# Two gates of five channel blocks by seven products, in one fused diffusion-transformer layer

## The chip, the core and the metric

One core of a Trainium2 chip. The kernel is one launch; its time is the device time in microseconds. TensorE (PE) multiplies, VectorE (DVE) and ScalarE (ACT) work elementwise, GpSimd (POOL) too, SyncE (SP) issues most loads. PEld is the loading of a matmul's stationary operand.

## The reference

One layer over x of 512 tokens by 1024 channels; everything is float32. The part that the change touches is the merge of three branches (Fourier f, convolution cv, attention at) under three gates, and the sums that give the modulation vectors:

```python
mod = jax.nn.silu(c) @ ada_w[l] + ada_b[l]
sh1, sc1, g1, sh2, sc2, g2 = jnp.split(mod, N_MOD, axis=-1)
hx = modulate(rmsnorm(x, norm1_g[l]), sh1, sc1)
px = split_proj(hx @ w_in[l])          # px[7], px[8], px[9]: the three gates, 1024 wide each
m = (jax.nn.sigmoid(g_f) * (f @ w_f) + jax.nn.sigmoid(g_c) * (cv @ w_c)
     + jax.nn.sigmoid(g_a) * (at @ w_a))
x = x + g1 * (m @ w_o)
x = x + g2 * sq_relu_mlp(modulate(rmsnorm(x, norm2_g[l]), sh2, sc2), mlp_w1[l], mlp_w2[l])
return rmsnorm(x, final_g)
```

## The kernel before

Every operand of a product is split into a high and a low part (split: ACT casts the high one, L59, DVE subtracts the low one, L60), and one product of a 128x128 weight piece with 512 tokens is three matmuls (mm3: L82 high by high, L83 high by the moving low, L84 the weight's low by the moving high). Weights come in 512 KB loads (weights(), L65 on SP) into two raw tiles (wraw) and are split into three tiles (wsp).

The stages in time: norm and values to 100 us, Fourier, convolution and attention to 241, the gates and merge to 402, output projection wO and second norm to 470, MLP to 790. In the attention, head() puts turns (four transposes tp and the split into pth and ptl, L421) on a list called pending, and output() (the matmuls po) closes a head; the three gates of block 0 are computed in between as filler, and drain() runs what is left.

The gate stage runs over 8 channel blocks c of 128 channels. In each, three gates of 24 matmuls of 512 columns (pg, moving operand hx), a sigmoid each on ACT, a merge of 24 (pbr, 6 for f, 6 for cv, 12 for at), products and sums on DVE (L536 to L538), and a split into mT. Among them DVE does 32 modulation units (ada_unit, L513): a 128x1024 block of ada_w, times a column of sig, added to acc, four vectors q of eight k each: q = 0 is g1, 1 the shift and 2 the scale of norm 2, 3 is g2. They start from a memset of acc on POOL (L507). In the first half of wO (py, four quarters kk, weights loaded by L65), a spread per q sums acc over the partitions by matmuls with ones (4 each).

In the MLP, two hidden blocks at a time are already computed by seven products (class Pair): with the moving operand and the weights cut in two by two quarters, seven products of quarter sums stand in for eight, each of 12 matmuls of 256 columns. The weights' sums are made by POOL (L768 to L773) and split again.

The order on each engine follows the written program, except that a scheduling layer moves instructions of one engine ahead of others that would wait. Buffers of a pool are reused in turn, so a load waits for the last reader of its tile.

Of the kernel before, what the change touches and what calls it, by code (L numbers as in the profile page):

```python
# [10 lines left out]
F32 = mybir.dt.float32  # L11
# [26 lines left out]
def dit_block(ctx: ExitStack, tc: tile.TileContext, a: dict):  # L38
# [16 lines left out]
    def f(ap):  # L55
        return ap.bitcast(F32)
# [345 lines left out]
    def head(p, j, q, bt, ats):  # L402
# [111 lines left out]

    ada_todo = [(k, q) for q in range(4) for k in range(KD)]
    for c in range(KD):
        pgs = []
        for b in range(3):
            if c == 0:
                sg = raw_gates[b]  # L520
                S.activation(sg, sg, AF.Sigmoid)
            else:
                pg = psG.tile([P, 512], F32, tag="g", name="pg")
                proj(pg, weights(a["wG"][c, b]))
                sg = (gp if c % 2 else sgp).tile([P, SEQ], F32, tag="sg", name="sg")
                S.activation(sg, pg, AF.Sigmoid)  # L526
            pgs.append(sg)
            ada_unit(*ada_todo.pop(0))
        w = weights(a["wM"][c])
        pbs = []  # L530
# [331 lines left out]
    def finish(pd, t, lo, n):  # L862
# [29 lines left out]
    for j, p in pairs.items():  # L892
# [150 lines left out]
```

## Time and profile before

| | us |
|---|---|
| median of 3 runs (804.94 to 805.08) | 805.07 |
| the profiled execution, its own time | 804.62 |
| its span, first to last instruction | 802.8 |
| PE busy | 783.9 |
| DVE busy | 528.2 |
| ACT busy | 347.0 |
| POOL busy | 110.6 |

The span is 1.8 us below the profiled execution's time, which holds what lies around the instructions. Busy times are of the whole span; what a stage is limited by is read from the windows of that stage. The durations of matmuls overlap: a matmul's cost is the distance between two starts.

### The profile page before, as it was taken

The page shows a single profiled execution, that of the slowest core. Times are in us where ns is not written, and L with a number is a line of the kernel's source. Part 1 is how long each engine was busy: PE and PEld are TensorE (multiplying, and loading weights), DVE is VectorE, ACT ScalarE, POOL GpSimd, SP SyncE. Part 2 cuts the span into 40 slices and gives each one's busy share as a digit, 9 for nine tenths or more (in the row PEclk, how much of TensorE's full clock was granted, in tenths as well). Part 3 has the DMA queues.
Part 4 walks back from the last instruction along what each step waited for, and adds up shares of the span by engine and source line. Part 5 has one row for each costly group of instructions (what it writes and reads, how often), then busy time and mean ns, then how long its engine had stood idle before and what let it go on. Part 6 is the DMA issues. An engine that isn't in the chain of part 4 may idle for free.

```text
span 802.8 us, 11393 instructions
## 1 busy us (share of the span) xinstructions
PE 783.9 (98%) x4484; PEld 674.4 (84%) x4484; DVE 528.2 (66%) x792; ACT 347.0 (43%) x587; POOL 110.6 (14%) x124
## 2 busy tenths in 40 slices
PE   5999999999999999999999999999999999999996
PEld 4779988788878888888888999999889989998885
DVE  4555445997888888543358988656556666475963
ACT  5434435564772222322245475344543444334232
POOL 1000011221210000000000005222221222032000
PEclk9999999999999999999999999999999999999999
DMA  8653242332308897322444142223233333221312
GB/s 342 249 198 94 84 126 67 85 94 79 83 28 296 311 324 248 131 83 102 151 146 150 39 146 80 86 99 110 101 106 106 106 105 105 105 79 53 119 65 106
DMA packets 33528, 104.07 MB, mean 130 GB/s; under 512 B 8001, under 2 KB 8129, under 8 KB 33473
## 3 DMA queue, kind: packets, MB, share of 16 engines
q1 hardware_dynamic: 32834, 100.99, 36.8%
q0 software_dynamic: 640, 2.36, 1.5%
q8 instruction: 35, 0.57, 0.3%
q14 instruction: 19, 0.16, 0.1%
HBM read 98.87 MB, written 2.10 MB: 126 GB/s over the span
## 4 chain that ended last, share of the span: by engine, by line
PE 94%; DVE 2%; ACT 1%; issue 1%; DMA 1%; SPq 0%; POOLq 0%; POOL 0%; ACTq 0%
PE pd L82 7%; PE pd L83 7%; PE pd L84 7%; PE pg L84 5%; PE pg L83 5%; PE pg L82 5%; PE pA L84 3%; PE pA L83 3%; PE pA L82 3%; PE pu L83 2%; PE pu L82 2%; PE pu L84 2%; PE pbr L83 2%; PE pbr L84 2%; PE pbr L82 2%; PE vacc L82 2%
## 5 line engine op out<-in xcount | busy, mean ns | idle before, releaser
L60 DVE TENSOR_TENSOR w<-raw,w 128x1024 fp32r<-128x1024 f32 x87 | 108.1, 1243 | 51.7 <-ACT w L59 51.7
L59 ACT CAST w<-raw 128x1024 fp32r<-128x1024 f32 x87 | 91.2, 1048 | 75.9 <-PE pbr L84 27.7
L60 DVE TENSOR_TENSOR w<-rr,w 128x512 fp32r<-128x512 f32 (+1 forms) x65 | 66.6, 1044 | 70.8 <-ACT w L59 69.6
L83 PE MATMUL pd<-w,aT 128*128 128x512 f32 x224 | 87.8, 392 | 0.0
L84 PE MATMUL pd<-w,aT 128*128 128x512 f32 x224 | 87.6, 391 | 0.0
L82 PE MATMUL pd<-w,aT 128*128 128x512 f32 x224 | 85.8, 394 | 0.0
L59 ACT CAST w<-rr 128x512 fp32r<-128x512 f32 (+1 forms) x65 | 45.0, 707 | 77.2 <-POOL rr L772 34.7
L84 PE MATMUL pg<-hx,w 128*128 128x512 f32 x192 | 76.4, 398 | 0.0
L83 PE MATMUL pg<-hx,w 128*128 128x512 f32 x192 | 76.2, 397 | 0.0
L82 PE MATMUL pg<-hx,w 128*128 128x512 f32 x192 | 74.9, 390 | 0.0
L84 PEld LDWEIGHTS pd<-w,aT 128*128 128x128 f32 x224 | 42.0, 188 | 9.3
L83 PEld LDWEIGHTS pd<-w,aT 128*128 128x128 f32 x224 | 42.1, 188 | 8.9 <-DVE w L60 0.8
L82 PEld LDWEIGHTS pd<-w,aT 128*128 128x128 f32 x224 | 41.8, 188 | 8.2 <-ACT w L59 0.4
L513 DVE SCALAR_TENSOR_TENSOR acc<-ada,sig,acc 128x1024 f32<-128x1024 f32 x32 | 40.9, 1282 | 10.1 <-DMA ada<-in_adaB 9.6
L82 PEld LDWEIGHTS pg<-hx,w 128*128 128x128 f32 x192 | 36.8, 192 | 8.0
L83 PEld LDWEIGHTS pg<-hx,w 128*128 128x128 f32 x192 | 36.1, 188 | 7.9
L768 POOL TENSOR_TENSOR rr<-rr 128x512 f32<-128x512 f32 x13 | 17.3, 1332 | 183.4 <-DVE w L60 159.9
L84 PEld LDWEIGHTS pg<-hx,w 128*128 128x128 f32 x192 | 36.1, 188 | 7.3
L104 POOL TENSOR_TENSOR ss<-ss,mhalf 128x1 f32<-128x1 f32 x10 | 6.6, 658 | 242.8 <-DVE ss L103 242.8
L526 ACT ACTIVATE sg<-pg 128x512 f32<-128x512 f32 x21 | 12.5, 597 | 62.2 <-PE pg L84 62.1
L536 DVE TENSOR_TENSOR sg<-pbr,sg 128x512 f32<-128x512 f32 x24 | 16.5, 686 | 20.6 <-PE pbr L84 20.6
L84 PE MATMUL pA<-Sq,w 128*128 128x256 f32 x104 | 29.3, 282 | 0.0
(337 smaller groups left out, 2152.1 us busy)
## 6 DMA issues: line engine op xcount, KB each, us to landing
raw<-in_w SPq DMA_DIRECT2D x38, 512.0 KB, 3.4
ada<-in_adaB SPq DMA_DIRECT2D x32, 512.0 KB, 4.6
rr<-in_w SPq DMA_DIRECT2D x26, 512.0 KB, 4.0
raw<-in_wG SPq DMA_DIRECT2D x24, 512.0 KB, 3.4
raw<-in_adaA SPq DMA_DIRECT2D x16, 512.0 KB, 5.5
raw<-in_wM SPq DMA_DIRECT2D x8, 512.0 KB, 3.4
raw<-in_wO SPq DMA_DIRECT2D x8, 512.0 KB, 3.3
raw<-in_wC SPq DMA_DIRECT2D x6, 512.0 KB, 3.3
```

Of the source, the lines that this page charges most:

```text
L59: S.copy(hi, src)
L60: V.tensor_tensor(lo, src, f(hi), op=ALU.subtract)
L82: PE.matmul(out, st[0], mv[0], start=start, stop=False, **kw)
L83: PE.matmul(out, st[0], mv[1], start=False, stop=False, **kw)
L84: PE.matmul(out, st[1], mv[0], start=False, stop=stop, **kw)
L104: G.tensor_tensor(ss, ss, mhalf[:, 0:n], op=ALU.pow)
L513: V.scalar_tensor_tensor(acc[:, q, :], raw, sigv[:, k, 0:1], acc[:, q, :], op0=ALU.mult, op1=ALU.add)
L526: S.activation(sg, pg, AF.Sigmoid)
L536: V.tensor_tensor(pgs[b], pb, pgs[b], op=ALU.mult)
L768: G.tensor_tensor(ra[:, lo], ra[:, lo], rb[:, lo], op=ALU.add)
```

## The change

For blocks 0 to 2 the gates stay as they are. For blocks 3 to 7 (FIRST = 3) the first two gates are computed as one pair of seven products, 84 matmuls of 256 columns (class Gates) in place of 48 of 512; the third gate and the merge keep theirs. Four quarter sums of hx (Sg0 to Sg3, gate_sums) are made on DVE and split during blocks 0 to 2, in memory of acc and of tiles that the pairs use later. Each pair has four additions of 128x512 on POOL for the weights' sums. The products run in the order gA, gC, gB, gA, gC, and then among the merge's parts: pbr of f, p7, pbr of cv, p4, pbr of at. The merge weights of these blocks lie in rows of mT that aren't filled yet, and those of block 7 in the two ada tiles.

The memset of acc is gone: the unit k = 0 of a vector writes acc (TENSOR_SCALAR, L520), and POOL's queue adds the bias to one partition by an accumulating load. Units are pinned to the written order; q = 3 (g2) moves to the MLP, eight units in pairs 4 to 11 and a spread in pair 13. Six units are left for after block 7. There are two ada tiles, before three. At the end of attention, the last output() goes through the list, and the last two turns are set into the middle of gate 2 of block 0.

The core of the diff:

```diff
...
-            if jb == 3:
+            if jb == 3 and (p, j) == (3, 1):
+                later(lambda: output(p, j, pth, ptl, ats))
+            elif jb == 3:
                 output(p, j, pth, ptl, ats)
...
-    def raw_gate(b):
+    def raw_gate(b, midway=None):
...
-        proj(pg, weights(a["wG"][0, b]))
+        w = weights(a["wG"][0, b])
+        proj(pg, w, ks=range(0, 4))
+        if midway:
+            midway()
+        proj(pg, w, ks=range(4, KD))
...
-            raw_gate(2)
+            raw_gate(2, lambda: [pending.pop(0)() for _ in range(2)])
...
-    gp = pool(gg, "gp", 3)
+    gp = pool(gg, "gp", 2)
+    gq = pool(gg, "gq", 1)
     psG = pool(gg, "psG", 8, space=PSUM)
-    G.memset(acc, 0.0)
-    nc.sync.dma_start(acc[0:1], a["adab"])
...
     def ada_unit(k, q):
         raw = gp.tile([P, D], F32, tag="ada", name="ada")
         nc.sync.dma_start(raw, a["adaB"][q, k])
-        V.scalar_tensor_tensor(acc[:, q, :], raw, sigv[:, k, 0:1], acc[:, q, :], op0=ALU.mult, op1=ALU.add)
...
-    ada_todo = [(k, q) for q in range(4) for k in range(KD)]
+        if k:
+            unit = V.scalar_tensor_tensor(acc[:, q, :], raw, sigv[:, k, 0:1], acc[:, q, :], op0=ALU.mult, op1=ALU.add)
+        else:
+            unit = V.tensor_scalar(acc[:, q, :], raw, sigv[:, 0, 0:1], None, op0=ALU.mult)
+        tc.keep_in_program_order(unit)
+        if k == 0:
+            G.dma_start(acc[0:1, q, :], a["adab"][:, q, :], accum_op=ALU.add)
...
+    ada_todo = [(0, q) for q in (0, 2, 1)] + [(k, q) for q in (0, 2, 1) for k in range(1, KD)]
...
+    def ada_some(n):
+        for _ in range(min(n, len(ada_todo))):
+            ada_unit(*ada_todo.pop(0))
...
+    def gate_sums():
...
+        whole(u, quarter(1, 0))
+        yield
+        whole(v, quarter(1, 1))
+        V.tensor_tensor(v, v, u, op=ALU.subtract)
+        keep(0, v)
+        yield
+        whole(w, quarter(0, 0))
+        V.scalar_tensor_tensor(v, v, -1.0, w, op0=ALU.mult, op1=ALU.subtract)
...
+        whole(w, quarter(0, 1))
+        V.scalar_tensor_tensor(w, v, -1.0, w, op0=ALU.mult, op1=ALU.subtract)
+        keep(3, w)
...
+    class Gates:
...
+        def __init__(self, c, sgs):
...
+            self.ra = wraw.tile([P, RAW], F32, tag="raw", name="ra")[:, :D]
+            nc.sync.dma_start(self.ra, a["wG"][c, 0])
+            self.rb = gq.tile([P, D], F32, tag="rb", name="rb")
+            nc.sync.dma_start(self.rb, a["wG"][c, 1])
+        def weights(self):
+            ra, rb = self.ra, self.rb
+            self.w1 = wsp.tile([P, 2, RAW], F32R, tag="w", name="w")
+            split(self.w1[:, 0, :D], self.w1[:, 1, :D], ra)
+            lo, hi = slice(0, 512), slice(512, 1024)
+            G.tensor_tensor(ra[:, lo], ra[:, lo], rb[:, lo], op=ALU.add)
+            self.b22 = gq.tile([P, 2, 512], F32R, tag="b22", name="b22")
+            split(self.b22[:, 0], self.b22[:, 1], rb[:, hi])
+            G.tensor_tensor(rb[:, lo], rb[:, lo], rb[:, hi], op=ALU.add)
+            G.tensor_tensor(rb[:, hi], ra[:, lo], rb[:, hi], op=ALU.add)
+            G.tensor_tensor(ra[:, hi], ra[:, hi], rb[:, hi], op=ALU.add)
+            self.w2 = wsp.tile([P, 2, RAW], F32R, tag="w", name="w")
+            split(self.w2[:, 0, lo], self.w2[:, 1, lo], ra[:, lo])
+            split(self.w2[:, 0, hi], self.w2[:, 1, hi], rb[:, hi])
...
+        def last_weights(self):
...
+            self.w3 = wsp.tile([P, 2, RAW], F32R, tag="w", name="w")
+            split(self.w3[:, 0, lo], self.w3[:, 1, lo], rb[:, lo])
+            split(self.w3[:, 0, hi], self.w3[:, 1, hi], ra[:, hi])
...
+        def first_products(self):
+            self.A, self.C, B = [psG.tile([P, 512], F32, tag="g", name=n) for n in ("gA", "gC", "gB")]
+            r0, r1 = self.sgs
+            self.product(self.A, self.w1, 0, quarter(0, 0), True)
+            a1 = self.copy("e1", self.A)
+            self.product(self.C, self.w2, 0, self.sq(0), True)
+            self.a5 = self.copy("e5", self.C)
+            self.product(B, self.w1, 512, quarter(0, 1), True)
+            V.tensor_tensor(r0[:, :HT], B[:, :HT], a1, op=ALU.add)
+            S.activation(r0[:, :HT], r0[:, :HT], AF.Sigmoid)
+            self.product(self.A, self.w2, 512, self.sq(1), False)
+            a2 = self.copy("e2", self.A)
+            self.last_weights()
+            self.product(self.C, self.b22, 0, self.sq(3), False)
+            V.tensor_tensor(r1[:, :HT], self.C[:, :HT], a2, op=ALU.add)
...
+        def p7(self):
+            r1 = self.sgs[1]
+            self.product(self.A, self.w3, 0, self.sq(2), False)
+            V.tensor_tensor(r1[:, HT:], self.A[:, :HT], self.a5, op=ALU.add)
+            S.activation(r1, r1, AF.Sigmoid, scale=-1.0)
+        def p4(self):
+            self.product(self.A, self.w3, 512, quarter(1, 1), False)
+            S.activation(self.sgs[0][:, HT:], self.A[:, :HT], AF.Sigmoid)
...
+    FIRST = 3
...
+    def merge_weights(c):
...
+        if c < FIRST:
+            w = weights(a["wM"][c])
+            return [[w[:, h, k * P:(k + 1) * P] for h in range(2)] for k in range(KD)]
+        raw = wraw.tile([P, RAW], F32, tag="raw", name="raw")
+        nc.sync.dma_start(raw[:, :D], a["wM"][c])
+        if c < KD - 1:
+            w = [mT[:, :, KD - 1 - h, :] for h in range(2)]
+        else:
+            w = [gp.tile([P, D], F32R, tag="ada", name="wm").rearrange("p (i n) -> p i n", i=2) for _ in range(2)]
+        split(w[0], w[1], raw[:, :D].rearrange("p (i n) -> p i n", i=2))
+        return [[w[h][:, k // 4, (k % 4) * P:(k % 4 + 1) * P] for h in range(2)] for k in range(KD)]
...
+    sums = gate_sums()
...
+        pair = c >= FIRST
+        for b in (2,) if pair else range(3):
+            if c in (1, 2):
+                next(sums, None)
...
+            if not pair:
+                ada_some(1)
+        if pair:
+            gates = Gates(c, pgs[:2])
+            gates.weights()
+            w = merge_weights(c)
+            gates.first_products()
+            ada_some(1 if c < KD - 1 else 0)
...
         for b, (k0, n, src) in enumerate(((0, 2, fT), (2, 2, cvT), (4, 4, atT))):
...
             for k in range(n):
-                mm3(pb, [w[:, h, (k0 + k) * P:(k0 + k + 1) * P] for h in range(2)],
-                    [src[:, h, k, :] for h in range(2)], k == 0, k == n - 1)
-            V.tensor_tensor(pgs[b], pb, pgs[b], op=ALU.mult)
+                mm3(pb, w[k0 + k], [src[:, h, k, :] for h in range(2)], k == 0, k == n - 1)
+            if pair and b < 2:
+                (gates.p7, gates.p4)[b]()
+            if pair and b < 1:
+                first = pb
+                continue
+            if b == 1 and pair:
+                V.tensor_tensor(pgs[1], pb, pgs[1], op=ALU.mult)
+                V.tensor_tensor(pgs[0], first, pgs[0], op=ALU.mult)
+            else:
+                V.tensor_tensor(pgs[b], pb, pgs[b], op=ALU.mult)
         V.tensor_tensor(pgs[0], pgs[0], pgs[1], op=ALU.add)
         V.tensor_tensor(pgs[0], pgs[0], pgs[2], op=ALU.add)
         split(mT[:, 0, c, :], mT[:, 1, c, :], pgs[0])
-        ada_unit(*ada_todo.pop(0))
+        ada_some((1, 0, 0, 1, 1, 1, 1, 24)[c])
...
-        q = (0, 2, 1, 3)[i]
+        q = (0, 2, 1)[i]
...
+        if kk < 3:
+            spread(kk)
...
+    G.memset(g2b, 0.0)
+    nc.sync.dma_start(g2b[0:1], a["adab"][:, 3, :])
...
+    def g2_unit(k):
+        raw = wraw.tile([P, RAW], F32, tag="raw", name="raw")[:, :D]
+        nc.sync.dma_start(raw, a["adaB"][3, k])
+        V.scalar_tensor_tensor(g2b, raw, sigv[:, k, 0:1], g2b, op0=ALU.mult, op1=ALU.add)
...
+        if 4 <= j < 12:
+            g2_unit(j - 4)
+        if j == 13:
+            g2_spread()
...
```

Three places of the order. The first is DVE from the last attention output (atT) to the low half of the weights of block 1's third gate (w_2573 before, w_2593 after). Numbers tell buffers apart; hx, u, w_2512 and Sg belong to the quarter sums. Before:

```order
L60 TENSOR_TENSOR atT_90<-ats_2129,atT_90 128x512
L536 TENSOR_TENSOR sg_2127<-pbr_2463,sg_2127 128x512
L513 SCALAR_TENSOR_TENSOR acc_2437<-ada_2447,sig_78,acc_2437 128x1024
L536 TENSOR_TENSOR sg_2356<-pbr_2471,sg_2356 128x512
L513 SCALAR_TENSOR_TENSOR acc_2437<-ada_2451,sig_78,acc_2437 128x1024
L537 TENSOR_TENSOR sg_2127<-sg_2127,sg_2356 128x512
L513 SCALAR_TENSOR_TENSOR acc_2437<-ada_2455,sig_78,acc_2437 128x1024
L536 TENSOR_TENSOR sg_2388<-pbr_2479,sg_2388 128x512
L60 TENSOR_TENSOR w_2573<-raw_2571,w_2573 128x1024
```

After (rows of block 0's merge are left out):

```order
L60 TENSOR_TENSOR atT_90<-ats_2129,atT_90 128x512
L550 TENSOR_TENSOR u_2511<-hx_88 128x1024
L520 TENSOR_SCALAR acc_2437<-ada_2452,sig_78 128x1024
L699 TENSOR_TENSOR sg_2127<-pbr_2471,sg_2127 128x512
...
L558 TENSOR_TENSOR acc_2437<-acc_2437,u_2511 128x1024
...
L60 TENSOR_TENSOR Sg0_2447<-acc_2437,Sg0_2447 128x1024
...
L550 TENSOR_TENSOR w_2512<-hx_88 128x1024
...
L518 SCALAR_TENSOR_TENSOR acc_2437<-ada_2505,sig_78,acc_2437 128x1024
L562 SCALAR_TENSOR_TENSOR acc_2437<-acc_2437,w_2512 128x1024
L518 SCALAR_TENSOR_TENSOR acc_2437<-ada_2545,sig_78,acc_2437 128x1024
L60 TENSOR_TENSOR Sg1_2448<-acc_2437,Sg1_2448 128x1024
...
L60 TENSOR_TENSOR w_2593<-raw_2591,w_2593 128x1024
```

Between atT and that split stood 7 rows; now 18 do: the quarter sums' five wide instructions and L562 have come in, and the units stand among them.

The second is DVE around block 4's merge. Before (w_3048 are the merge weights, w_3091, w_3126 and w_3161 the three gates of block 5):

```order
L60 TENSOR_TENSOR w_3048<-raw_3046,w_3048 128x1024
L60 TENSOR_TENSOR w_3091<-raw_3089,w_3091 128x1024
L536 TENSOR_TENSOR sg_2971<-pbr_3051,sg_2971 128x512
L60 TENSOR_TENSOR w_3126<-raw_3124,w_3126 128x1024
L536 TENSOR_TENSOR sg_3006<-pbr_3059,sg_3006 128x512
L537 TENSOR_TENSOR sg_2971<-sg_2971,sg_3006 128x512
L536 TENSOR_TENSOR sg_3041<-pbr_3067,sg_3041 128x512
L538 TENSOR_TENSOR sg_2971<-sg_2971,sg_3041 128x512
L60 TENSOR_TENSOR w_3161<-raw_3159,w_3161 128x1024
```

After, from the last splits of block 4's pair (w_3131) to L637, on which the pair's last product p4 waits, and the first product of its merge; w_3222 is the third gate of block 5, ra_3250 and rb_3252 are the raw weights of block 5's pair:

```order
L60 TENSOR_TENSOR w_3131<-rb_3051,w_3131 128x512
L60 TENSOR_TENSOR w_3131<-ra_3049,w_3131 128x512
L626 TENSOR_TENSOR sg_3015<-gB_3074,e1_3087 128x256
L60 TENSOR_TENSOR w_3222<-raw_3220,w_3222 128x1024
L632 TENSOR_TENSOR sg_3016<-gC_3073,e2_3129 128x256
L518 SCALAR_TENSOR_TENSOR acc_2437<-ada_3149,sig_78,acc_2437 128x1024
L60 TENSOR_TENSOR w_3254<-ra_3250,w_3254 128x1024
L60 TENSOR_TENSOR b22_3258<-rb_3252,b22_3258 128x512
L637 TENSOR_TENSOR sg_3016<-gA_3072,e5_3101 128x256
L696 TENSOR_TENSOR sg_3016<-pbr_3173,sg_3016 128x512
```

L637 has come in, behind a unit and two splits of the next pair; the merge's first product L536 (now L696) waits behind it.

The third is SP's queue at the start of wO. Before:

```order
L65 DMA raw<-in_wM 128x1024
L65 DMA raw<-in_wO 128x1024 x3
L564 DMA x_3535<-in_x 128x1024 x3
L561 DMA a2b<-in_norm_g 128x1024
L564 DMA x_3535<-in_x 128x1024
L65 DMA raw<-in_wO 128x1024
```

After:

```order
L654 DMA raw<-in_wM 128x1024
L65 DMA raw<-in_wO 128x1024 x3
L516 DMA ada<-in_adaB 128x1024 x2
L727 DMA x_3840<-in_x 128x1024
L516 DMA ada<-in_adaB 128x1024 x2
L727 DMA x_3840<-in_x 128x1024 x2
L516 DMA ada<-in_adaB 128x1024 x2
L727 DMA x_3840<-in_x 128x1024
L65 DMA raw<-in_wO 128x1024
```

Before, all units were done by then; now six unit loads and all x loads stand ahead of the fourth quarter of wO.

## Rows read from the trace of the kernel before

**Rows 1.** The page: busy time of each engine, and the chain by engine.
```profile
PE 783.9 (98%) x4484; PEld 674.4 (84%) x4484; DVE 528.2 (66%) x792; ACT 347.0 (43%) x587; POOL 110.6 (14%) x124
...
PE 94%; DVE 2%; ACT 1%; issue 1%; DMA 1%; SPq 0%; POOLq 0%; POOL 0%; ACTq 0%
```

**Rows 2.** Windows: length, busy us of each engine, clock, DMA share, GB/s.
```profile
225.00:241.00 16.00, 14.06 (x79) 11.20 (x78) 12.45 (x26) 10.79 (x21) 3.53 (x1) 1.00 0.11 35
243.00:270.00 27.00, 27.00 (x119) 22.08 (x118) 23.93 (x25) 7.34 (x10) 0.00 (x0) 1.00 0.91 319
270.00:404.00 134.00, 134.00 (x582) 109.70 (x581) 79.78 (x85) 38.27 (x49) 0.00 (x0) 1.00 0.53 183
404.00:427.00 23.00, 23.00 (x102) 18.80 (x101) 13.85 (x17) 10.76 (x15) 0.00 (x0) 1.00 0.43 147
427.00:470.00 43.00, 42.76 (x264) 37.72 (x263) 39.53 (x60) 21.60 (x41) 3.07 (x4) 1.00 0.23 76
```

**Rows 3.** Timeline of the end of attention: start, duration, instruction, [idle before, releaser].
```profile
228.30 3.53 POOL L507 MEMSET acc<- 128x4096 f32 x1 [12.98 <-issue]
...
230.21 1.90 DVE L444 TENSOR_SCALAR pr<-pr,mx 128x512 f32<-128x512 f32 x1
...
232.25 0.52 PE L421 MATMUL tp<-ident,pr 128*128 128x128 f32 x3 [0.83 <-DVE pr L444]
...
238.24 0.50 PE L452 MATMUL po<-pth,Vst 128*128 128x512 f32 x1 [0.78 <-ACT pth L59]
239.07 0.50 PE L452 MATMUL po<-ptl,Vst 128*128 128x512 f32 x1 [0.33 <-DVE ptl L60]
...
240.79 0.39 PE L82 MATMUL pbr<-fT,w 128*128 128x512 f32 x1
```

**Rows 4.** Windows of PE alone: one block of the MLP's products, one gate block.
```profile
487.62:499.05 11.43, 11.43 (x98) 1.00 0.35 120
333.00:355.18 22.18, 22.18 (x97) 1.00 0.29 95
```

**Rows 5.** Line L444: duration in ns, minimum/median/maximum, first and last start.
```profile
L444 DVE TENSOR_SCALAR pr<-pr,mx x32: 467/479/1898, 133.8 to 233.9; 128x512 f32<-128x512 f32 x32
```

**Rows 6.** Timeline of DVE at the start of the gates.
```profile
243.04 0.69 DVE L60 TENSOR_TENSOR atT<-ats,atT 128x512 fp32r<-128x512 f32 x1 [0.69 <-ACT atT L59]
...
244.89 1.28 DVE L513 SCALAR_TENSOR_TENSOR acc<-ada,sig,acc 128x1024 f32<-128x1024 f32 x1 [0.56 <-DMA ada<-in_adaB]
246.09 0.68 DVE L536 TENSOR_TENSOR sg<-pbr,sg 128x512 f32<-128x512 f32 x1
...
249.68 0.68 DVE L536 TENSOR_TENSOR sg<-pbr,sg 128x512 f32<-128x512 f32 x1
250.28 1.22 DVE L60 TENSOR_TENSOR w<-raw,w 128x1024 fp32r<-128x1024 f32 x1
251.42 0.69 DVE L538 TENSOR_TENSOR sg<-sg 128x512 f32<-128x512 f32 x1
```

**Rows 7.** Line L150, a wide DVE instruction with one SBUF tensor.
```profile
L150 DVE TENSOR_SCALAR xt<-xt,ss x6: 742/753/771, 7.8 to 26.3; 128x1024 f32<-128x1024 f32 x6
```

**Rows 8.** Loads: a unit load's first issue; KB each and median us to landing.
```profile
240.98 1.31 SPq L512 DMA_DIRECT2D ada<-in_adaB  x3
...
ada<-in_adaB SPq DMA_DIRECT2D x32, 512.0 KB, 4.6
...
q<-q POOLq DMA_DIRECT2D x8, 288.0 KB, 3.0
```

**Rows 9.** Timelines of POOL and of DVE in an MLP pair.
```profile
512.49 1.28 POOL L768 TENSOR_TENSOR rr<-rr 128x512 f32<-128x512 f32 x1 [11.47 <-DVE w L60]
513.85 1.63 POOL L771 TENSOR_TENSOR rr<-rr 128x512 f32<-128x512 f32 x1
...
512.66 1.67 DVE L60 TENSOR_TENSOR b<-rr,b 128x512 fp32r<-128x512 f32 x1
```

**Rows 10.** Lines of ACT from 382 to 430: busy, mean ns, idle before.
```profile
L59 ACT CAST w<-acc 128x1024 fp32r<-128x1024 f32 x4 | 4.2, 1046 | 10.4 <-PE py L84 10.4
```

More of the change, by code (lines that the diff above doesn't have):

```diff
@@ L252, in dit_block, with proj @@
     g1.close()
-    def proj(ps, w, src=hx):
-        for k in range(KD):
+    def proj(ps, w, src=hx, ks=range(KD)):
+        for k in ks:
             mm3(ps, [w[:, h, k * P:(k + 1) * P] for h in range(2)], [src[:, h, k, :] for h in range(2)],
@@ new lines, in ada_unit, with quarter @@
+        tc.keep_in_program_order(unit)
[5 more added lines that the diff above has]
+            ada_unit(*ada_todo.pop(0))
+    def quarter(i, j):
+        return [hx[:, h, 4 * j:4 * j + 4, i * HT:(i + 1) * HT] for h in range(2)]
+    Sg = [gq.tile([P, 2, 4, HT], F32R, name=f"Sg{i}") for i in range(4)]
@@ new lines, in half_tile, with whole, keep @@
+    def half_tile(n):
+        return n.rearrange("p (k t) -> p k t", t=HT)
+    def gate_sums():
+        u = half_tile(gq.tile([P, D], F32, tag="rb", name="u"))
+        v = half_tile(acc[:, 3, :])
+        w = half_tile(gq.tile([P, D], F32, tag="b22", name="w"))
+        def whole(dst, q):
+            V.tensor_tensor(dst, f(q[0]), f(q[1]), op=ALU.add)
+        def keep(i, src):
+            split(Sg[i][:, 0], Sg[i][:, 1], src)
+        whole(u, quarter(1, 0))
[6 more added lines that the diff above has]
+        V.scalar_tensor_tensor(v, v, -1.0, w, op0=ALU.mult, op1=ALU.subtract)
+        keep(1, v)
+        yield
+        V.tensor_tensor(u, w, u, op=ALU.subtract)
+        keep(2, u)
+        yield
+        whole(w, quarter(0, 1))
+        V.scalar_tensor_tensor(w, v, -1.0, w, op0=ALU.mult, op1=ALU.subtract)
+        keep(3, w)
@@ new lines, in dit_block, with product, sq, copy @@
+    class Gates:
+        def __init__(self, c, sgs):
+            self.c, self.sgs = c, sgs
+            self.ra = wraw.tile([P, RAW], F32, tag="raw", name="ra")[:, :D]
[17 more added lines that the diff above has]
+        def last_weights(self):
+            ra, rb = self.ra, self.rb
+            lo, hi = slice(0, 512), slice(512, 1024)
+            self.w3 = wsp.tile([P, 2, RAW], F32R, tag="w", name="w")
+            split(self.w3[:, 0, lo], self.w3[:, 1, lo], rb[:, lo])
+            split(self.w3[:, 0, hi], self.w3[:, 1, hi], ra[:, hi])
+        def product(self, bank, w, lo, mv, start):
+            for k in range(4):
+                c = lo + k * P
+                mm3(bank[:, :HT], [w[:, h, c:c + P] for h in range(2)], [mv[h][:, k, :] for h in range(2)],
+                    start and k == 0, k == 3, skip_group_check=True)
+        def sq(self, i):
+            return [Sg[i][:, h] for h in range(2)]
+        def copy(self, tag, bank):
+            e = gq.tile([P, HT], F32, tag=tag, name=tag)
+            S.copy(e, bank[:, :HT])
+            return e
+        def first_products(self):
[21 more added lines that the diff above has]
+            S.activation(self.sgs[0][:, HT:], self.A[:, :HT], AF.Sigmoid)
@@ L519, in dit_block @@
+    sums = gate_sums()
+    for c in range(KD):
+        pgs = raw_gates if c == 0 else [
+            (gp if c % 2 and b < 2 else sgp).tile([P, SEQ], F32, tag="sg", name="sg") for b in range(3)]
+        pair = c >= FIRST
+        for b in (2,) if pair else range(3):
+            if c in (1, 2):
+                next(sums, None)
             if c == 0:
-                sg = raw_gates[b]
-                S.activation(sg, sg, AF.Sigmoid)
+                S.activation(pgs[b], pgs[b], AF.Sigmoid)
@@ L524, in dit_block @@
                 proj(pg, weights(a["wG"][c, b]))
[L525 to L530 removed]
+                S.activation(pgs[b], pg, AF.Sigmoid)
+            if not pair:
[7 more added lines that the diff above has]
+        else:
+            w = merge_weights(c)
         for b, (k0, n, src) in enumerate(((0, 2, fT), (2, 2, cvT), (4, 4, atT))):
@@ L872, in finish, with g2_spread @@
             V.tensor_tensor(xs, xs, fgb[:, :n], op=ALU.mult)
+    G.memset(g2b, 0.0)
[4 more added lines that the diff above has]
+        V.scalar_tensor_tensor(g2b, raw, sigv[:, k, 0:1], g2b, op0=ALU.mult, op1=ALU.add)
+    def g2_spread():
+        w = weight_tile()
+        split(w[:, 0, :D], w[:, 1, :D], g2b)
+        for n in range(2):
+            sl = slice(n * 512, (n + 1) * 512)
+            pg = psZ.tile([P, 512], F32, tag="b", name="pg", bufs=2)
+            for h in range(2):
+                PE.matmul(pg, ones, w[:, h, n * 512:(n + 1) * 512], start=(h == 0), stop=(h == 1))
+            S.copy(g2b[:, sl], pg)
     begun = [plain_start(0)]
```

7 lines of the change are left out of this document (2 added, 5 removed).

## The prediction

> **What bounds the kernel now.** I read the page's shares and its chain of waits first, then the windows stage by stage, then the places where TensorE stands still, and last what the vector engine (DVE), the loads and GpSimd (POOL) have left over. TensorE is busy for 98% of the span and carries 94% of the chain [rows 1]. From 243 us on, the windows show no hole in it through all the gates, and 0.24 us in the 43 us after the first half of wO; its clock is at the upper level, 1.00 [rows 2]. So this kernel's time is the TensorE work that is issued, plus the few stops. The change is therefore worth what it takes off TensorE's stream, less every new stop. The only stops near the change lie at the end of attention: of 16.00 us TensorE is busy 14.06 [rows 2], and three waits make up that 1.94: 0.83, 0.78 and 0.33 [rows 3]. DVE is the engine to watch: 23.93 of 27.00 us busy in the first 27 us of the gates, with the loads at 0.91 of their engines [rows 2].
>
> **What the seven products take off.** A whole block of the old form (three gates of 24 matmuls and a merge of 24, 96 in all, 512 columns each) takes 22.18 us, so 0.2311 us each; 96 matmuls of 256 columns in the MLP took 11.43 us, so 0.1191 us each (the window counts of 97 and 98 take in those that overlap its edges) [rows 4]. Two gates cost 48 x 0.2311 = 11.09 us; seven products of 12 cost 84 x 0.1191 = 10.00. The gain is 1.09 us per block, 5 blocks: **-5.5**. This is a small gain, 12.5% fewer columns and 10% less time, since the short matmuls carry more per column; and it is paid for with work on DVE, POOL and the loads. That is why I cost those closely.
>
> [...]
>
> **End of attention.** POOL's memset of acc began at 228.30 and took 3.53 us. While it ran, the normalisation at L444 took 1.90 us [rows 3], against 0.479 in the median of 32 [rows 5]; it ended 0.28 us after the memset did. Without the memset that is 1.42 us earlier, so the 0.83 us wait of the transposes goes. The other two waits come because the last two turns stand together and the last output() follows at once; now 5 gate matmuls (5 x 0.2311 = 1.16 us) stand between the last turn and output(), against 0.78 + 0.33 of waiting. The turns come earlier, so a few tenths may stay. **-1.7**, bounds -0.8 (the memset alone) and -1.94 (all).
>
> **Third gate of block 1.** In the gates' order this is the first new stop. Before, its low half (w_2573) was started at 250.28 us, after 8 rows from atT on; 72 matmuls behind the first pbr (240.79) TensorE wants it, at 257.4: 6 us to spare [rows 3, 6]. Now it stands 19 rows behind atT. Call the first pbr T0. DVE starts atT at T0 + 2.25 (243.04 - 240.79) [rows 3, 6]. Steps from start to start: a 1024-wide DVE instruction of two SBUF operands 1.14 (250.28 to 251.42), a modulation unit 1.20 (244.89 to 246.09), a 512-wide one 0.60 (249.68 to 250.28) [rows 6]; the new units for k = 0 have one SBUF operand, at about 0.68, from the 0.753 of a 1024-wide one [rows 7] less the overlap. So atT 0.60, six 512-wide of block 0's merge 3.6, five wide (three of them the sums' own adds, two the low halves of Sg0 and Sg1) 5.7, three k = 0 units 2.0, L562 and three L518 units 4.8, and 1.2 for the split itself: 17.9, so T0 + 20.2. TensorE has 72 matmuls and 8 it can take ahead: 80 x 0.2311 = 18.5. **+1.9.** The loads can lengthen this: there are two ada tiles in place of three, so the third unit's load starts only when the first unit is done; the first came 3.9 us after its issue [rows 6, 8], their median is 4.6 [rows 8]. Bounds 0 (the steps overlap better) and +3.2.
>
> The memset's replacement by an accumulating load from POOL's queue costs nothing here: the next unit of the same q comes three units later, more than the 3.0 us that the loads of that queue took [rows 8].
>
> **In each pair.** p4, the last product, waits for L637, since it adds to the bank that L637 reads. L637 in turn stands behind a modulation unit and two splits for the next block (ra, then rb's high half). From the end of gA's Sg2 product (p7), on which L637 depends, to p4, TensorE has cvT: 6 x 0.2311 = 1.39 us. From gC's end, on which L632 depends, it has fT, p7 and cvT: 1.39 + 1.43 + 1.39 = 4.2. DVE needs L632 0.34, unit 1.20, split 1.14, split 0.60, L637 0.42 and two handovers, 4.0. That is nearly level, and ra comes third in SP's queue after ada and rb. With 0.2 for each of the four pairs that have a next one: **+0.8**, bounds 0 and +4.8 (1.2 each).
>
> The upper bound is a lock that the trace shows: DVE's b split, 0.6 us alone, took 1.67 beside POOL's add at 512.49, ending 0.56 us after that add; the next add took 1.63 in place of 1.28, waiting for DVE in turn [rows 9]. Each pair here issues four such POOL adds. In the new order the b split follows ra's split with nothing between, while POOL's first add is released only by the end of ra's split, so I expect DVE first and POOL to pay. [...]
>
> **wO's fourth quarter.** Six modulation units are left for after block 7. Their two tiles hold block 7's merge weights, so their loads begin when the merge ends (T0'). First two land at about T0' + 3.9 [rows 6, 8]; each later load waits for a unit two before it. Unit times: 3.9 to 5.2, to 6.4; third 9.2 to 10.5; fourth (behind wO#3's split) 11.6 to 12.9; fifth 14.5 to 15.8; sixth 16.9 to 18.2. ACT casts acc for q = 1 first (1.05 [rows 10]) and wO#4 after, to T0' + 20.2, with the low half 1.14 later. TensorE has 72 matmuls and 8 spreads, 18.5 us; before, it lost nothing here [rows 2]. By this the stop is 1.7 for the high half and up to 1 for the low one; with loads at 3.4 us instead of 4 it is near 0.5. **+1.8**, bounds 0.5 and 3.
>
> **After it.** In 427 to 470 DVE is busy 39.53 of 43 us [rows 2], so what it brings along late is not caught up: a2b, residuals and norm2 shift. **+0.8**, bounds 0 and 2. The eight g2 units in the MLP and their spread (4 matmuls, moved, not added) hide behind TensorE, which is the bound there; if DVE were full they would cost 8 x 1.2 us.
>
> **Sum.** -5.5 - 1.7 + 1.9 + 0.8 + 1.8 + 0.8 = -1.9. The profiled execution took 804.62 us, 0.45 below the median of 805.07, so 802.7 for a profiled one and **803.2** for the median. A difference under 0.2% (1.6 us) cannot be told from none.
>
> **Rivals.**
> (a) The gain comes through: DVE and loads hold, only the -5.5 and -1.7 are seen, with under 1.5 us of stops. About 798 to 800. For it: TensorE's windows had no hole even at DVE 89%. Against: three counted chains are longer than their cover.
> (b) The stops eat it all: the splits and loads of wO and of block 1 at their upper ends (+3.2 and +3), the rest as reckoned: -7.2 + 6.2 + 0.8 + 0.8 = +0.6, 805.7. No change. For it: all three new chains start with cold loads.
> (c) Slower: POOL takes the lock ahead of the b split in each pair. L637 is then 1.07 us later, and so is p4; with the lateness of ra's load 1.4 per pair, 5.6 in place of 0.8, net +2.9, 808.0. It decides once p4 waits over 1.1 us per pair (4 x 1.1 - 0.8 = 3.6, which takes -1.9 above +1.6). For it: the 1.67 us [rows 9]. Against: the order of the two starts.
>
> **Chances.** The forecast (some -4 to 0) 0.55, (a) 0.15, (b) 0.17, (c) 0.13. Of the forecast a little over half lies beyond -1.6. Faster 0.48, same 0.32, slower 0.20 (of (c), and the upper edge of (b)). Range 799.0 to 807.5; the likeliest case alone 801 to 805.
>
> **What would show it.** 256-column gates at 0.119 us with no waits in blocks 3 to 7 would confirm the first term. L444 at 0.48 and no wait on it confirm the second. A wait of L84 pg on DVE w, L60, some 18.5 us after the first pbr of block 0, is the third; p4 on L637 the fourth; py on ACT w the fifth. I am wrong if the waits in the gates sum to under 1 or over 6 us, or if a stage that I called full, the MLP, shows holes.

## The result, and the profile after

The changed kernel takes 813.26 us (median of 4 runs, 812.18 to 814.99), the kernel before 805.01 in the same comparison (804.88 to 805.08): a ratio of 1.0105, 95% interval 1.0091 to 1.0119. It is slower by 8.2 us, where I forecast 1.9 faster, and lies outside my range. The profiled execution took 814.27 us (span 812.5) against 804.62 (span 802.8), so the traces show 9.7 us to explain.

The page of the changed kernel gives busy time and chain, the answers to [rows 1].

```profile
PE 784.5 (97%) x4664; PEld 680.8 (84%) x4664; DVE 561.9 (69%) x839; ACT 366.6 (45%) x631; POOL 142.9 (18%) x147
...
PE 79%; DVE 8%; DMA 5%; ACT 3%; issue 2%; POOL 1%; SPq 0%; POOLq 0%; ACTq 0%; DVEq 0%
```

TensorE's busy time grew by 0.6 us although it has fewer columns to stream, and its share of the chain fell from 94 to 79%. Both are clues: part of what it gained was spent at a lower clock, and other work now ends last in places. The view of its waits (in total, times, longest) lists the places; the first row, in the prologue, is not the change's.

```profile
PE rows L163 <- DVE sig L136: 8.3, 1, 8.3
PE pg L84 <- DVE w L60: 3.5, 1, 3.5
PE py L82 <- ACT w L59: 2.5, 1, 2.5
PE gA L82 <- DVE sg L637: 1.4, 2, 1.0
PE pB L82 <- ACT r L907: 1.1, 1, 1.1
PE pA L82 <- ACT e L980: 0.8, 1, 0.8
PE pu L83 <- DVE aT L60: 0.7, 1, 0.7
```

The second is the third gate of block 1, the third wO's fourth quarter, the fourth p4; the last three are the start of the MLP, which I had called full. The windows (columns as in [rows 2], TensorE alone here) show what follows a stop.

```profile
228.00:242.00 14.00, 14.00 (x79) 1.00 0.24 76
...
262.00:264.00 2.00, 2.00 (x8) 0.65 0.89 277
264.00:266.00 2.00, 2.00 (x6) 0.50 0.89 320
...
422.00:424.00 2.00, 1.16 (x3) 0.76 0.52 211
424.00:426.00 2.00, 2.00 (x6) 0.50 0.45 102
426.00:428.00 2.00, 2.00 (x10) 0.89 0.53 205
```

The end of attention is now without a hole (before, TensorE was busy for 12.06 us of the same window). But behind each of the two long stops the granted clock goes to 0.50, at 264 to 266 and at 424 to 426 us, while TensorE is busy for all of the 2.00 us. TensorE's timeline at the first stop shows what that costs.

```profile
257.23 0.39 PE L83 MATMUL pbr<-atT,w 128*128 128x512 f32 x1
261.12 0.50 PE L84 MATMUL pg<-hx,w 128*128 128x512 f32 x1 [3.51 <-DVE w L60]
261.46 0.40 PE L82 MATMUL pg<-hx,w 128*128 128x512 f32 x1
...
262.40 0.44 PE L83 MATMUL pg<-hx,w 128*128 128x512 f32 x1
262.64 0.63 PE L84 MATMUL pg<-hx,w 128*128 128x512 f32 x1
263.07 0.63 PE L82 MATMUL pg<-hx,w 128*128 128x512 f32 x1
...
265.20 0.63 PE L84 MATMUL pg<-hx,w 128*128 128x512 f32 x1
265.63 0.58 PE L82 MATMUL pg<-hx,w 128*128 128x512 f32 x1
```

The stop itself costs more than the 3.51 that is listed, since the record of a matmul (0.39) outlasts its pitch, the distance from start to start (0.23): 257.23 to 261.12 is 3.89, so 3.66 are lost, and the next matmul takes 0.34, another 0.1. The stops at p4, at wO and at the MLP's start likewise cost 0.2 to 0.3 more than their listed waits. After it TensorE runs at its pitch for some 1.3 us, then at 0.43 for some eight matmuls: about 1.6 us more. At wO nine matmuls take 3.76 us in place of 2.1, so 1.7 are lost there behind the stop.

```profile
422.84 1.94 PE L82 MATMUL py<-w,mT 128*128 128x512 f32 x4 [2.48 <-ACT w L59]
...
426.60 0.40 PE L83 MATMUL py<-w,mT 128*128 128x512 f32 x1
```

Starts of TensorE's stages, read from the timelines, sort the loss (us). vacc are the first matmuls of the values, ahead of everything that the change touches.

```
              first vacc  first pbr  first py  first pu  first pd   span
before           18.56      240.79    401.67    451.63    502.74    802.8
after            19.21      238.98    401.81    456.12    510.87    812.5
lost up to it    +0.65       -2.46     +1.95     +4.35     +3.65     +1.5
```

The 0.65 is not the change's: the longest wait of that stretch, at L163, is 7.9 us before and 8.3 after, and 7.8 to 8.8 over the 13 profiled kernels, which share it. The end of attention gains 2.5. The gates lose 2.0 where my terms for them come to 2.8 gained; in wO and norm2, 4.4 go; at the start of the MLP 3.7; in the rest 1.5.

### The profile page after: what moved, and what is told of

It is laid out like the page before. It is cut to its first block, busy times and chain, and to the rows that moved or that the text cites. A ratio compares the mean times of both kernels' runs of the same rounds, so it can differ in the third digit from the quotient of the medians.

```text
span 812.5 us, 11906 instructions
## 1 busy us (share of the span) xinstructions
PE 784.5 (97%) x4664; PEld 680.8 (84%) x4664; DVE 561.9 (69%) x839; ACT 366.6 (45%) x631; POOL 142.9 (18%) x147
## 4 chain that ended last, share of the span: by engine, by line
PE 79%; DVE 8%; DMA 5%; ACT 3%; issue 2%; POOL 1%; SPq 0%; POOLq 0%; ACTq 0%; DVEq 0%
PE pd L82 7%; PE pd L83 7%; PE pd L84 7%; PE pg L84 3%; PE pg L83 3%; PE pA L82 3%; PE pA L84 3%; PE pA L83 3%; PE pg L82 3%; DMA ada<-in_adaB 2%; DVE w L60 2%; PE vacc L82 2%; DMA ra<-in_wG 2%; PE tp L421 1%; PE pC L84 1%
## 5 line engine op out<-in xcount | busy, mean ns | idle before, releaser
L60 DVE TENSOR_TENSOR w<-raw,w 128x1024 fp32r<-128x1024 f32 x72 | 89.8, 1247 | 31.0 <-ACT w L59 31.0
L59 ACT CAST w<-raw 128x1024 fp32r<-128x1024 f32 x72 | 75.6, 1050 | 53.9 <-PE pd L84 12.0
L84 PE MATMUL pg<-hx,w 128*128 128x512 f32 x112 | 45.5, 406 | 3.5 <-DVE w L60 3.5
L83 PE MATMUL pg<-hx,w 128*128 128x512 f32 x112 | 45.1, 402 | 0.0
L82 PE MATMUL pg<-hx,w 128*128 128x512 f32 x112 | 44.5, 397 | 0.0
L59 ACT CAST aT<-r 128x512 fp32r<-128x512 f32 x32 | 19.9, 622 | 24.1 <-DVE r L998 24.0
L518 DVE SCALAR_TENSOR_TENSOR acc<-ada,sig,acc 128x1024 f32<-128x1024 f32 x21 | 26.9, 1279 | 5.0 <-DMA ada<-in_adaB 4.9
L82 PE MATMUL pA<-Sq,w 128*128 128x256 f32 x104 | 29.5, 284 | 0.8 <-ACT e L980 0.8
L84 PE MATMUL pA<-A,w 128*128 128x256 f32 x104 | 29.3, 282 | 0.0
L84 PE MATMUL pA<-Sq,w 128*128 128x256 f32 x104 | 29.3, 282 | 0.0
L83 PE MATMUL pA<-A,w 128*128 128x256 f32 x104 | 29.3, 282 | 0.0
L82 PE MATMUL pA<-A,w 128*128 128x256 f32 x104 | 29.3, 282 | 0.0
L83 PE MATMUL pA<-Sq,w 128*128 128x256 f32 x104 | 29.2, 281 | 0.0
```

The costliest lines, as they stand in the source:

```text
L59: S.copy(hi, src)
L60: V.tensor_tensor(lo, src, f(hi), op=ALU.subtract)
L82: PE.matmul(out, st[0], mv[0], start=start, stop=False, **kw)
L83: PE.matmul(out, st[0], mv[1], start=False, stop=False, **kw)
L84: PE.matmul(out, st[1], mv[0], start=False, stop=stop, **kw)
L518: unit = V.scalar_tensor_tensor(acc[:, q, :], raw, sigv[:, k, 0:1], acc[:, q, :], op0=ALU.mult, op1=ALU.add)
```

## The experiments

Times are medians; the ratio is to the kernel before in the same comparison, with its 95% interval. Edits are against the changed kernel unless said otherwise.

**1. Pairs undone.** Blocks 3 to 7 take their three gates as before; with that, units come three to a block again and merge weights lie where they lay. All else of the change stays.

```diff
-    FIRST = 3
+    FIRST = 8
```

> All edits but the pairs: every block's gates by 24 matmuls of 512 columns, the quarter sums still made (unused), the units done by block 6. Theory A (the loss lies in single stops at three places, and in TensorE's lower clock behind the two long ones): the 5.5 us of the pairs and their p4 waits are gone, the wO stop and the late MLP start too, the stop at block 1's third gate stays with its slow stretch, 3.5 + 1.6: 805.0 - 1.7 + 5.1 = 808.4 (807 to 810). Rival B (the pair blocks themselves lose it, by DVE and POOL in each other's way): 803 to 805.

Measured: 808.28 us (806.92 to 810.31), ratio 1.0037 (1.0025 to 1.005). The waits at wO, at p4 and at the MLP's start are gone, and of the new ones one stays, the third gate's:

```profile
PE pg L84 <- DVE w L60: 2.5, 1, 2.5
```

So the pairs, meant to save 5.5 us, cost 5.0 with all that hangs on them. By stages of the profiled executions the pairs gain 0.7 up to the first py, and lose 5.3 from there to the first pu and 3.5 more to the first pd. That the median meets theory A's number is partly luck. In the profiled execution (806.92) the stop was 2.5 and the clock did not fall behind it, where A had 3.5 + 1.6; and from the first pd to the end it took 302.3 us against 300.1 before, which A had not counted (the g2 units and their spread).

**2. Sums' first step later.** The stop at the third gate alone is aimed at.

```diff
-            if c in (1, 2):
+            if c in (1, 2) and (c, b) != (1, 0):
```

> The five steps of the quarter sums begin one gate later, so that the low half of block 1's third gate stands ahead of the second sum on DVE. A: the 3.5 us stop and the slow matmuls behind it go, 5.1 us in all, the rest stays: 808.2 (807 to 809.5). Rival C (the stop is made by the unit whose load came 1.78 us late with two ada tiles, and only half of it by the sums): 810.5 to 812.

Measured: 807.78 (805.06 to 810.3), ratio 1.0033 (1.0018 to 1.0047). The third gate's wait has left the list, and wO's stays at 2.2 us. In its profile the first py is at 394.6, 7.2 us earlier than in the changed kernel: some 3.8 is the stop, 1.6 the clock, 1.9 the two stops on L637, which are gone too though the edit does not touch them. The order of DVE's queue set the stop.

**3. Units earlier.** Units move ahead of the last block, so that few are left at wO.

```diff
-        ada_some((1, 0, 0, 1, 1, 1, 1, 24)[c])
+        ada_some((1, 0, 0, 3, 3, 2, 2, 24)[c])
```

> The six units left for after block 7 are done at the ends of blocks 3 to 6 (two more in 3 and 4, one more in 5 and 6). A: the stop at wO's fourth quarter and its slow stretch go (4.3 us), and so does the late MLP start that follows from it (some 3 us); up to 1 us more for p4: 806 to 807.5. Rival D (the MLP starts late because the eight units of g2 and their loads are there now): only 4.3 go, 809 to 810.

Measured: 811.0 (810.25 to 814.13), ratio 1.0077 (1.0055 to 1.0098). Neither number held. The wait at wO is gone and the MLP's start is normal again (first pu to first pd 51.4 us, 51.1 before, 54.8 after), so both went with wO's late units (what decides at the MLP is taken up below). But a pair now stands still: the timelines of SP, ACT and TensorE read as one chain.

```profile
369.20 1.65 SPq L516 DMA_DIRECT2D ada<-in_adaB  x2
371.72 0.33 SPq L578 DMA_DIRECT2D ra<-in_wG  x1
```

```profile
378.23 1.04 ACT L59 CAST w<-ra 128x1024 fp32r<-128x1024 f32 x1 [5.48 <-DMA ra<-in_wG]
```

```profile
381.52 0.58 PE L82 MATMUL gA<-hx,w 128*128 128x256 f32 x1 [4.54 <-DVE sg L637]
```

ra's load is issued behind two unit loads and ACT finds it only at 378.23; L637 stands behind the split of ra on DVE, and p4 behind L637. The cost was moved, not removed.

**4. p4 later.** p4 comes behind the merge's last product, so that L637 has twelve matmuls more.

```diff
-            if pair and b < 2:
-                (gates.p7, gates.p4)[b]()
+            if pair and b != 1:
+                (gates.p7, None, gates.p4)[b]()
...
+            elif pair:
+                V.tensor_tensor(pgs[2], pb, pgs[2], op=ALU.mult)
```

> The last product of a pair, p4, stands behind the attention part of the merge in place of the convolution part: 12 matmuls more, 2.8 us, for L637. A: the two waits on L637 go, 1.4 us, and nothing else changes: 811.9 (811 to 813). If the MLP's late start is a matter of the order of its loads on SP (here the pair's raw weights stand ahead of the fourth plain weight again, as before the change) and not of what is inherited: 808 to 810.

Measured: 811.18 (808.76 to 811.83), ratio 1.0064 (1.0044 to 1.0084). No wait on L637 is left, but wO's grew from 2.5 to 4.9 us. TensorE comes to wO 4.2 us sooner in the profiled execution, the end of the last unit only 1.6. That the median lies near A's 811.9 is luck, since much else changed: the third gate's stop was 2.6 with no slow stretch, first py to first pu grew by 2.9, and first pu to first pd fell from 54.8 to 52.0.

**5. wO's loads first.** The loads of all four quarters are issued ahead of the six units, and the fourth's split stands ahead of the third spread.

```diff
+        if c == KD - 1:
+            wos = [weights(a["wO"][0, kk]) for kk in range(3)]
+            raw3 = wraw.tile([P, RAW], F32, tag="raw", name="raw")
+            nc.sync.dma_start(raw3[:, :D], a["wO"][0, 3])
         ada_some((1, 0, 0, 1, 1, 1, 1, 24)[c])
...
-        w = weights(a["wO"][0, kk])
+        w = wos[kk]
...
+        if kk == 2:
+            w = weight_tile()
+            split(w[:, 0, :D], w[:, 1, :D], raw3[:, :D])
+            wos.append(w)
```

> The load of wO's fourth quarter is issued ahead of the six unit loads left after block 7, and its split stands ahead of the third spread; the units stay where they are. A: the stop at the fourth quarter and its slow stretch go, 4 us; of the MLP's late start (3.7 us) what comes from the norm's lateness goes too, some 1.5: 807 to 809.5 from 813.3. Rival E (the six units on DVE are the delay, not the load's place in the queue): only 1 us less, 812.

Measured: 808.34 (805.29 to 811.01, 7 runs), ratio 1.0042 (1.0026 to 1.0058). No wait at wO; 2.2 at the third gate, 0.9 and 0.7 at the MLP's start, which stays late (first pu to first pd 53.9).

**6. Edits of 2, 4 and 5 together.**

> Sums one gate later, p4 behind the attention part of the merge, and wO's fourth load ahead of the units. A: the three stops and their slow stretches go, the MLP starts on time; what is left of the change is -5.5 for the pairs and -1.7 at the end of attention, against some +1 for the g2 units in the MLP: 799 (797.5 to 801). Rival B (the pair blocks are too dense on DVE and POOL, and a stop removed comes back elsewhere): 803 to 806.

Measured: 800.63 (799.1 to 802.34), ratio 0.9943 (0.9931 to 0.9956). Apart from MLP starts under 1 us, one new stop is left, on TensorE's timeline, with ACT's at the same place:

```profile
417.43 1.22 PE L740 MATMUL pg<-w,ones 128*128 128x512 f32 x4 [2.90 <-ACT g1b L754]
```

```profile
413.32 1.05 ACT L59 CAST wo<-raw 128x1024 fp32r<-128x1024 f32 x1 [5.71 <-DMA raw<-in_wO]
415.85 1.04 ACT L59 CAST wo<-raw 128x1024 fp32r<-128x1024 f32 x1 [1.48 <-DMA raw<-in_wO]
416.80 1.07 ACT L754 COPY g1b<-pg 128x512 f32<-128x512 f32 x2
```

The second spread wants a PSUM bank that the copy to g1b frees, and ACT holds that copy behind two casts whose loads come late.

**7. The attention part alone, on the kernel before.** The late output(), the turns amid the gate, and no memset; the code of the gates stays old.

```diff
+            if jb == 3 and (p, j) == (3, 1):
+                later(lambda: output(p, j, pth, ptl, ats))
...
-            raw_gate(2)
+            raw_gate(2, lambda: [pending.pop(0)() for _ in range(2)])
...
-    G.memset(acc, 0.0)
-    nc.sync.dma_start(acc[0:1], a["adab"])
...
+            V.tensor_scalar(acc[:, q, :], raw, sigv[:, 0, 0:1], None, op0=ALU.mult)
+            G.dma_start(acc[0:1, q, :], a["adab"][:, q, :], accum_op=ALU.add)
```

> The kernel before with two edits of the change alone: the last output() through the list with the last two turns inside gate 2 of block 0, and no memset (the k = 0 units write acc and the bias is added by POOL's queue). The term of the prediction: -1.7, so 803.4 (803.1 to 804.2). Rival F (the accumulating loads hold up the unit loads, and the start of the gates loses what the end of attention gains): 805 or more.

Measured: 802.46 (802.18 to 802.94), ratio 0.9966 (0.9954 to 0.9978): 2.9 us gained, where my term was 1.7. TensorE is busy for all of the window from 228 to 242.

**8. Without the accumulating loads.**

```diff
-            G.dma_start(acc[0:1, q, :], a["adab"][:, q, :], accum_op=ALU.add)
+            pass
```

> The change without the three accumulating loads: the bias of three modulation vectors is left out. If they made the third unit's load late (5.3 us to land where the first took 3.9), the wait of 1.78 us on DVE and about as much of the stop at block 1's third gate go: 811 or less. A: the load is late because two more loads are under way and is not helped: 813.

Measured: 810.03 (807.23 to 812.47), ratio 1.0059 (1.0038 to 1.0079). DVE's wait for the third unit's load is 0.34 us here and 1.78 in the profile after. But experiments 5 and 6, with these loads, show 0.47 and 0.74, so this landing varies by itself, and the run settles nothing on them.

**9. A bank of its own for the second spread**, on top of 6.

```diff
-        pg = psZ.tile([P, 512], F32, tag="a", name="pg", bufs=2)
+        pg = psZ.tile([P, 512], F32, tag="b" if q == 2 else "a", name="pg", bufs=2)
```

> The version with all three stops taken away, and the spread of the norm's scale summed in two PSUM banks of its own, so that it doesn't wait for the copies of g1. A: the 2.9 us stop that the former version had there goes: 797.7 (796.5 to 799). Rival: the third spread takes the wait over, and it is as before, 800.6.

Measured: 800.27 (800.08 to 800.89), ratio 0.9942 (0.9929 to 0.9954). The stop shrank from 2.90 to

```profile
417.33 0.73 PE L740 MATMUL pg<-w,ones 128*128 128x512 f32 x2 [1.04 <-ACT w L59]
```

and the profiled span from 800.5 to 799.1, but the median by 0.4 only; I expected 797.7. This is the best version that does the whole work, and it beats both kernels.

**10. Kernel 9 with the pairs undone** (FIRST = 8).

> That version without the pairs: all gates by 24 matmuls of 512 columns, everything else alike, the quarter sums made and unused. The term of the prediction: the pairs take 5.5 us off TensorE, so 803.2 if the version with pairs takes 797.7. Rival B (the pairs give most of it back on DVE and POOL even where no long stop is left): 800 or less, that is under 2.5 us apart.

Measured: 804.36 (803.67 to 804.75, 11 runs), ratio 0.9988 (0.9979 to 0.9997). The pairs are worth 4.1 us; up to the first py, 5.2 (394.5 against 399.7), of which wO gives some back. But kernel 9 is only 2.2 us faster than experiment 7, which has the attention part alone: what makes room for the pairs, without them, costs 1.9 (804.36 against 802.46).

**11. Kernel 9 without the g2 units and their spread.**

```diff
-        if 4 <= j < 12:
-            g2_unit(j - 4)
-        if j == 13:
-            g2_spread()
```

> That version without the eight g2 units and their spread in the MLP: g2 is its bias alone. The spread is 4 matmuls of 0.23 us on TensorE, 0.9 us, and is the same before and after the change, in another place. A: 0.9 to 1.1 us less than the version with them. Rival: the units' loads and DVE work cost TensorE more there, 2 us or more.

Measured: 798.67 (797.71 to 799.32), ratio 0.9923 (0.991 to 0.9937): 1.6 us less than kernel 9. Four matmuls of the spread account for 0.9, so the units' own cost in the MLP is some 0.7 us by the medians, neither nothing nor 2. From the first pd to the end, the profiled executions took 302.2 us in kernel 9 and 300.1 here, which gives 1.1.

## Why the prediction failed, point by point

**Seven products: -5.5, right.** In experiments 9 and 10 the first pbr to the first py takes 155.5 and 160.9 us, 5.4 less with the pairs, and in the changed kernel their blocks show no stop but p4's.

**End of attention: -1.7, undersized.** All of the 1.94 us of waits [rows 3] went, as my upper bound had it. From the first vacc to the first pbr it is 222.2 us before, 219.8 after and 219.5 in experiment 7, so 2.5 to 2.7 gained (2.9 by the medians of experiment 7). The part above 1.94 is the cost of a stop beyond its listed wait: the 0.33 in [rows 3], for one, stands between two starts 0.83 apart.

**Third gate: +1.9, measured 3.5 and the clock; the steps right, the load left out.** DVE's timeline behind the first pbr (238.98, T0) shows the counted units and splits up to the one that TensorE wants, and one wait among them.

```profile
243.07 0.75 DVE L520 TENSOR_SCALAR acc<-ada,sig 128x1024 f32<-128x1024 f32 x1
...
249.18 0.75 DVE L520 TENSOR_SCALAR acc<-ada,sig 128x1024 f32<-128x1024 f32 x1 [1.78 <-DMA ada<-in_adaB]
...
258.66 1.28 DVE L518 SCALAR_TENSOR_TENSOR acc<-ada,sig,acc 128x1024 f32<-128x1024 f32 x1
259.85 1.22 DVE L60 TENSOR_TENSOR w<-raw,w 128x1024 fp32r<-128x1024 f32 x1
```

The split ends at 261.07, T0 + 22.1; I had T0 + 20.2, and nearly all of the difference is the wait of 1.78. (20.2 less the 18.5 of TensorE is 1.7; the +1.9 of the prediction is 0.2 above its own steps.) SP's timeline has that load's issue:

```profile
239.17 0.80 SPq L516 DMA_DIRECT2D ada<-in_adaB  x2
240.07 0.38 SPq L65 DMA_DIRECT2D raw<-in_wM  x1
243.84 16.45 SPq L516 DMA_DIRECT2D ada<-in_adaB  x6
```

It is issued at 243.84, when the first unit frees its tile, and the unit starts 5.3 us later; I used the 3.9 of the first load, and had the longer one in the bounds only (+3.2, passed by 0.3). Over the runs the stop follows this wait one to one: waits of 0.34, 0.47, 0.80, 0.92 and 1.78 us (experiments 8, 5, 1, 4 and the changed kernel) go with stops of 2.1, 2.2, 2.5, 2.6 and 3.5, so 1.7 or 1.8 of each is DVE's queue, as predicted. Experiment 2 removed it by order alone.

**p4: +0.8, measured 1.4**, in two of the four pairs. Experiment 4 shows that a later place of p4 removes it. What made L637 late at the longer one is ra's load, as ACT's timeline shows; DVE's b split and POOL's additions are at the same place.

```profile
373.14 1.05 ACT L59 CAST w<-ra 128x1024 fp32r<-128x1024 f32 x1 [2.89 <-DMA ra<-in_wG]
375.37 0.69 DVE L60 TENSOR_TENSOR b<-rb,b 128x512 fp32r<-128x512 f32 x1
375.58 1.61 POOL L587 TENSOR_TENSOR ra<-ra,rb 128x512 f32<-128x512 f32 x1 [16.29 <-DVE w L60]
377.27 1.29 POOL L590 TENSOR_TENSOR rb<-rb 128x512 f32<-128x512 f32 x1
```

Rival (c), POOL taking the lock ahead of the b split, has no support: it needed over 1.1 us in each pair and the longest wait is 1.0; and DVE started first here, its split took 0.69, and POOL's addition took 1.61 where the next took 1.29, the order that I expected.

**wO's fourth quarter: +1.8, found at its place; 2.5.** ACT's timeline, T0' = 401.8:

```profile
420.61 1.04 ACT L59 CAST w<-acc 128x1024 fp32r<-128x1024 f32 x1 [10.11 <-DVE acc L518]
421.75 1.04 ACT L59 CAST w<-raw 128x1024 fp32r<-128x1024 f32 x1
```

The cast of wO ends at T0' + 21.0; I had 20.2. The cast did not wait for its own load but stood behind that of acc, as predicted. Experiment 5, which moved the load and the split together, removed the stop.

**The step that failed most: what a stop costs, and "after it".** I priced a stop at its own length. Behind the two long ones the clock fell to 0.50, +1.6 and +1.7, a term that the prediction does not have, and each stop cost 0.2 to 0.3 more than its listed wait. And "after it" was +0.8, bounds 0 and 2, with the start of the MLP held to be full; it came to 0.6 (a transpose, L804, listed 0.5) and then 3.7 up to the first pd. Holes in the MLP were one of my signs of being wrong. The windows there (all engines), where the kernel before has TensorE busy for all 20.00 us of each, and SP's timeline:

```profile
480.00:500.00 20.00, 18.89 (x157) 18.48 (x156) 12.71 (x14) 12.82 (x23) 6.32 (x4) 1.00 0.38 130
500.00:520.00 20.00, 19.23 (x136) 17.93 (x136) 14.42 (x19) 9.41 (x18) 5.49 (x4) 1.00 0.46 163
```

```profile
455.44 26.32 SPq L65 DMA_DIRECT2D raw<-in_w  x4
482.69 16.22 SPq L920 DMA_DIRECT2D rr<-in_w  x5
```

SP's loads went out in the order in which they stand: the four of L65 took from 455.44 to 481.76, and the rr loads came behind them. Before, the first pair's rr loads went out ahead of the fourth plain weight's load:

```profile
472.59 1.66 SPq L756 DMA_DIRECT2D rr<-in_w  x3
475.92 0.33 SPq L65 DMA_DIRECT2D raw<-in_w  x1
```

Now that plain weight's load stands ahead of them and waits for its tile, and the first rr load goes out at 482.69, some 10 us later (5.6 of them when counted from the first pu), and ACT waits for it:

```profile
487.80 1.05 ACT L59 CAST w<-rr 128x1024 fp32r<-128x1024 f32 x1 [3.13 <-DMA rr<-in_w]
```

I read the order of instructions around wO and the gates but not the MLP's, where the diff has little. Over the runs the MLP's start goes with this order of loads, and not with late units at wO. Where the plain weight's load stands ahead (the changed kernel, experiments 2, 5 and 8), first pu to first pd takes 53.9 to 54.8 us. Where the rr loads do (before and the other eight experiments), it takes 51.1 to 52.2. Among these are 4, 6, 9 and 11, whose six units stay at wO; SP's timeline in experiment 4:

```profile
477.72 1.28 SPq L922 DMA_DIRECT2D rr<-in_w  x3
480.00 0.33 SPq L65 DMA_DIRECT2D raw<-in_w  x1
```

So the stop at wO is not what makes the MLP start late: 5 has no such stop and a late start, 4 the longest and a nearly normal one. No run moves that load alone, so this rests on the grouping of the 13 kernels and not on an edit.

**The g2 units: called hidden; 0.7 to 1.1** (experiment 11), and the spread's 0.9 moved from wO's stage into the last one, most of the 1.5 that this one lost.

Summed from the starts of matmuls in the profile after: -5.4 for the pairs, -2.5 at the end of attention, +3.8 and +1.6 at the third gate, +1.9 at p4, +2.7 and +1.7 at wO, +0.6, +3.7, +1.5 in the last stage, less 0.9 for the spread that left wO's stage, and 0.65 ahead of the change: +9.4 of 9.7. Rival (b), the stops eating it all, had the direction right but its sum stopped at 805.7, since it too had no clock and no MLP in it.

## What to carry to other kernels

When an edit puts more work behind a full engine, price each new stop with what follows it, not only with its length, and remove the stop by order: three small moves of order (sums, p4, wO's loads) turned 813.3 us into 800.6 in experiment 6. Read the order of every queue that the moved loads share to the end of the program, not to the end of the diff. And move work into the gaps that an engine has, with the loads counted: units moved from wO into the pairs (experiment 3) cost nearly as much there.

## What the runs showed of the hardware

In the profiles the granted clock fell to 0.50 behind stops of 2.1 and 2.9 (experiment 8), 2.2 (2), 2.5 and 3.5 (the changed kernel), 3.7 (3), and behind or within stops of 4.5 (3) and 4.9 us (4). It stayed at 1.00 behind stops of 2.2 (5), 2.5 (1), 2.6 (4) and 2.9 us (6). So between 2.1 and 2.9 us a stop's length alone does not tell what follows it, and what does stays open. It fits that executions of kernels with long stops scatter over 5 us (experiment 5, 805.29 to 811.01, mean granted clock 0.993 to 0.998) where those of kernel 9, with one stop of 1.0, scatter over 0.8 (clock 0.997 to 0.999).

A load's landing varied as well: the third unit's load, with the same loads ahead of it on SP, made DVE wait between 0.34 and 1.78 us (experiment 8 and the changed kernel), and experiment 8 could not tell why.
